# Queueing the state updates of linear attention as one alternating burst per half-head

## The chip, the cores and the metric

The kernel runs on one core of a Trainium2 chip. The metric is the device time of one execution, in microseconds (us). The chip's engines have queues of their own and meet only at semaphores: PE (TensorE, matrix products into PSUM), DVE (VectorE), ACT (ScalarE), POOL (GpSimd) and SP (SyncE, which here issues most of the transfers).

## The reference

Two layers of a hybrid encoder trunk on 512 frames of width 2048, all in float32. Each layer normalises its input, projects it with one wide matrix, and feeds two groups of heads: chunked softmax attention (8 heads of 128) and gated linear attention (4 heads, key width 128, value width 256). Gated outputs of both are concatenated, projected by `w_out`, normalised and added to the residual. The change concerns linear attention, which works in 8 chunks of 64 frames:

```python
L = jnp.cumsum(log_a..., axis=2)                 # inside a chunk
k_dec = kf * jnp.exp(L_end[:, :, None] - L)
U = jnp.einsum('bnchk,bnchv->bnhkv', k_dec, vf)  # one 128x256 update per chunk and head
A = jnp.exp(L_end)
new = a[..., None] * state + u                   # scan over the chunks
o = jnp.einsum('bnchk,bnhkv->bnchv', qf, states) # every frame reads its chunk's state
```

## The kernel before

The large projections run as matrix products on operands split into a high and a low part; each true product is kept as three (high·high, high·low, low·high). Weights are streamed from DRAM, ACT casts the high part (`wh`, L218), DVE subtracts the low part (`wl`, L223), and PE consumes them in jobs of 12 matmuls (in the blocks that save products, `fast_gemm`, L427 and L417) or 24 (`std_gemm`, L341). Between these, *tasks* add small work: attention, forget gates, linear attention, sums of operands for later products.

The program is built with a scheduler (the call passes `schedule_with_timeline_sim=True`): it decides, for each engine's queue, where an instruction stands, so the order of statements is only one of its inputs. `tc.issue_after(x)` makes what is recorded inside stand behind `x`. Engines then work through their queues strictly in that order, and a wait at the head of a queue holds all behind it.

Linear attention is cut into eight *units* per layer, one for a head `h` and a half `p` of the frames (256 frames, four chunks). `gla_heads` (behind the projection of the values, `gv_consume`) walks through two heads at a time. Units are numbered 0 to 7 here in the order in which they run: units 0 to 3 are heads 2 and 3, units 4 to 7 heads 0 and 1. For a unit:

- `outer` takes two PSUM banks, `ps_u[0]` and `ps_u[1]`, from a pool of four (`aux`), and forms the four chunk updates. A chunk has 64 frames, so its keys and values fill 64 of 128 partitions: chunk `cc` = 0 the lower half of the rows, `cc` = 1 the upper half. For each pair of chunks `tt` and each `cc`, three split products of 64 rows by 256 columns are accumulated into one half of bank `ps_u[cc]`: 12 matmuls (L1090).
- `states` is the scan on DVE: a copy (L1109) or four multiply-adds (L1111), which read the updates from PSUM.
- `read` has four matmuls of the queries with the states (L1124; each is unsplit float32 and shows as two in the trace) into a third bank.
- `norm` squares on ACT (L1134, L469) and takes a root on POOL (L465); `gate` multiplies on DVE (L1142); `turn`, delayed by some steps, transposes on PE (four matmuls, L1152) into another bank, which ACT copies out (L1163). Transfers then carry the result out and back for the sums of the output projection (L629, L655, L659; added on DVE at L622).

With four banks, the next `outer` waits until earlier banks have been read.

Of the kernel before, what the change touches and what calls it, by code (L numbers as in the profile page):

```python
# [34 lines left out]
def hybrid_trunk(  # L35
# [13 lines left out]
    nc = tc.nc  # L49
# [38 lines left out]
    def aux():  # L88
        return ps_ax.tile([P, 512], F32, tag="ax", name=nm("ax"))
# [620 lines left out]
    def layer(l):  # L710
# [359 lines left out]
        class Unit:  # L1070
# [5 lines left out]
            def outer(self):  # L1076
                h, p = self.h, self.p
                hk = slice(h * P, (h + 1) * P)
                hv = slice((h % 2) * 256, (h % 2 + 1) * 256)
                self.ps_u = [aux(), aux()]  # L1080
                for tt in range(2):
                    ops = []
                    for cc in range(2):
                        r = slice(cc * 64, (cc + 1) * 64)
                        kh, kl = kdh[p][r, tt, hk], kdl[p][r, tt, hk]
                        vh, vl = self.gvh[p][r, tt, hv], self.gvl[p][r, tt, hv]
                        ops.append(((kh, vh), (kh, vl), (kl, vh)))
                    for i in range(3):
                        for cc in range(2):
                            nc.tensor.matmul(  # L1090
                                self.ps_u[cc][:, tt * 256 : (tt + 1) * 256], ops[cc][i][0], ops[cc][i][1],
                                start=(i == 0), stop=(i == 2),
                            )

            def states(self):
                h, p = self.h, self.p
# [313 lines left out]
```

## Time and profile before

| what | value |
|---|---|
| time, median of 3 runs | 1637.59 us (1635.76 to 1638.52) |
| the profiled execution | 1637.15 us |
| its span | 1635.2 us |
| PE busy | 1625.8 us (99% of the span), 8990 matmuls |
| DVE, ACT, POOL busy | 1228.0, 904.6, 169.9 us |
| transfers | 469.59 MB, mean 287 GB/s |
| matmuls of `outer` (L1090) | 192, 26.5 us busy |

A matmul's busy time in the trace is longer than its share of PE, since matmuls overlap: two rows that follow each other start nearer together than the first one's duration. What a matmul costs is therefore read from the starts: the time from the start of one row to the start of a later one, divided among the instructions between them. A row of the timeline merges equal neighbours and gives their start, the time to the last one's end, and their count. Linear attention runs from about 590 to 690 us in the first layer and from about 1404 to 1504 us in the second.

### The profile page before, as it was taken

Reading aid. Unit: us, or ns where it says so; the run is one execution under the profiler, and the core shown is the slowest. Engines: PE = TensorE matmul, PEld = TensorE weight load, DVE = VectorE, ACT = ScalarE, POOL = GpSimd, SP = SyncE. Lnnn points to the kernel's source line nnn. Section 1 sums busy time; section 2 is a strip of 40 time slices with the busy share of each in tenths; the row PEclk is TensorE's granted clock in tenths of the full one; section 3 lists DMA queues with packets and bytes.
Section 4 is the critical chain, followed back from the end, with each engine's and each line's share of the span. In section 5 each row is a group of like instructions: output and inputs, shape, how many; then the busy total and the mean of one; then the engine's idle time right before and its main releaser. Section 6 shows DMA issues by size and latency. Waiting matters only on the chain.

```text
span 1635.2 us, 24844 instructions
## 1 busy us (share of the span) xinstructions
PE 1625.8 (99%) x8990; PEld 1392.6 (85%) x8990; DVE 1228.0 (75%) x1587; ACT 904.6 (55%) x1516; POOL 169.9 (10%) x259
## 2 busy tenths in 40 slices
PE   9999999999999999999999999999999999999998
PEld 7888889999978877788888888899999888777886
DVE  7567776877877886778886676768778778866887
ACT  8444544556676644555783445445566665445553
POOL 1210000001101201310122000000001012013100
PEclk9999999999999999999999999999999999999999
DMA  9979786858868696898789697968588676969986
GB/s 374 360 280 322 283 313 227 304 181 311 291 196 283 208 378 233 308 364 315 276 303 388 228 332 268 321 221 304 187 312 274 218 265 232 355 225 332 376 307 233
DMA packets 150778, 469.59 MB, mean 287 GB/s; under 512 B 16428, under 2 KB 35892, under 8 KB 150656
## 3 DMA queue, kind: packets, MB, share of 16 engines
q1 hardware_dynamic: 128064, 389.69, 68.1%
q0 software_dynamic: 22016, 77.37, 12.0%
q8 instruction: 71, 1.16, 0.3%
q10 hardware_dynamic: 576, 0.95, 0.2%
q14 instruction: 51, 0.42, 0.1%
HBM read 395.83 MB, written 71.06 MB: 286 GB/s over the span
## 4 chain that ended last, share of the span: by engine, by line
PE 99%; DMA 0%; DVE 0%; ACT 0%; SPq 0%; DVEq 0%; POOLq 0%; issue 0%
PE mm L427 46%; PE mm L341 22%; PE mm L417 20%; PE ax L920 2%; PE ax L1090 1%; PE ax L427 1%; PE ax L903 1%; PE ax L1124 1%; PE ax L745 1%; PE ax L882 1%; PE ax L883 1%; PE ax L881 1%; PE ax L1152 0%; PE ax L569 0%; PE ax L951 0%; DMA raw<-in_w_dram 0%
## 5 line engine op out<-in xcount | busy, mean ns | idle before, releaser
L427 PE MATMUL mm<-wh,sa 128*128 128x512 f32 x1536 | 485.1, 391 | 0.0
L218 ACT CAST wh<-raw 128x1024 fp32r<-128x1024 f32 x255 | 269.1, 1057 | 255.7 <-PE mm L427 115.8
L223 DVE TENSOR_TENSOR wl<-raw,wh 128x1024 fp32r<-128x1024 f32 (+1 forms) x257 | 312.3, 1217 | 125.5 <-PE mm L427 44.1
L218 ACT CAST wh<-H 128x1024 fp32r<-128x1024 f32 x224 | 235.3, 1053 | 217.6 <-PE mm L427 109.9
L223 DVE TENSOR_TENSOR wl<-H,wh 128x1024 fp32r<-128x1024 f32 x224 | 273.1, 1222 | 106.6 <-PE mm L427 46.4
L427 PEld LDWEIGHTS mm<-wh,sa 128*128 128x128 f32 x1536 | 287.9, 188 | 62.2 <-issue 1.5
L427 PE MATMUL mm<-wl,sa 128*128 128x512 f32 x768 | 299.9, 390 | 0.0
L417 PE MATMUL mm<-sa,wh 128*128 128x256 f32 x1280 | 237.3, 286 | 0.0
L417 PEld LDWEIGHTS mm<-sa,wh 128*128 128x128 f32 x1280 | 199.9, 191 | 0.3
L427 PE MATMUL mm<-wh,a 128*128 128x512 f32 x576 | 185.7, 393 | 0.0
L417 PE MATMUL mm<-sa,wl 128*128 128x256 f32 x640 | 180.6, 283 | 0.0
L427 PEld LDWEIGHTS mm<-wl,sa 128*128 128x128 f32 x768 | 144.3, 188 | 30.3
L341 PE MATMUL mm<-wh,a 128*128 128x512 f32 x512 | 167.4, 394 | 0.1
L207 DVE TENSOR_TENSOR H<-H,raw 128x1024 f32<-128x1024 f32 x120 | 145.9, 1220 | 3.5 <-DMA raw<-in_w_dram 1.8
L465 POOL TENSOR_TENSOR sm<-sm,mhalf 128x4 f32<-128x4 f32 (+2 forms) x40 | 60.6, 1514 | 777.7 <-DVE sm L936 550.8
L427 PEld LDWEIGHTS mm<-wh,a 128*128 128x128 f32 x576 | 107.9, 188 | 23.2 <-issue 0.8
L417 PEld LDWEIGHTS mm<-sa,wl 128*128 128x128 f32 x640 | 122.3, 191 | 0.1
L341 PEld LDWEIGHTS mm<-wh,a 128*128 128x128 f32 x512 | 96.0, 188 | 21.1 <-ACT wh L215 0.5
L427 PE MATMUL mm<-wl,a 128*128 128x512 f32 x288 | 113.0, 392 | 0.0
L341 PE MATMUL mm<-wl,a 128*128 128x512 f32 x256 | 100.1, 392 | 0.0
L417 PE MATMUL mm<-a,wh 128*128 128x256 f32 x512 | 94.9, 285 | 0.0
L341 PE MATMUL mm<-wh,sa 128*128 128x512 f32 x256 | 85.9, 394 | 0.0
(208 smaller groups left out, 2332.9 us busy)
## 6 DMA issues: line engine op xcount, KB each, us to landing
raw<-in_w_dram SPq DMA_DIRECT2D x319, 512.0 KB, 5.8
sa<-S SPq DMA_DIRECT2D x192, 512.0 KB, 4.7
H<-in_w_dram SPq DMA_DIRECT2D x56, 512.0 KB, 5.2
sa<-A SPq DMA_DIRECT2D x48, 512.0 KB, 6.1
S<-g POOLq DMA_DIRECT2D x32, 512.0 KB, 7.6
oS<-g POOLq DMA_DIRECT2D x32, 512.0 KB, 6.3
sa<-oS SPq DMA_DIRECT2D x32, 512.0 KB, 5.2
sg<-t POOLq DMA_DIRECT2D x32, 256.0 KB, 6.1
```

The costliest lines, as they stand in the source:

```text
L207: nc.vector.tensor_tensor(out=h, in0=h, in1=r, op=ALU.add)
L218: last_cast[0] = nc.scalar.copy(self.wh, src).ins
L223: last_low[0] = nc.vector.tensor_tensor(out=self.wl[:, kk, :], in0=self.src[:, kk, :], in1=self.wh[:, kk, :].bitcast(F32), op=ALU.subtract ...
L341: mm = nc.tensor.matmul(pss[o], a[:, part, t], rhs[:, kk, :], start=(i == 0 and kk == 0 and m == 0), stop=(i == n - 1 and kk == 1 and m == 2),
L417: nc.tensor.matmul(dst, lhs[:, kk, f], a[:, part, tok], start=(fresh and kk == 0 and m == 0 and ft % 2 == 0), stop=(c == c_last and kk == ...
L427: nc.tensor.matmul(out_ps[t], a[:, part, tok], rhs[:, kk, :], start=(fresh and kk == 0 and m == 0), stop=(c == c_last and kk == 1 and m == ...
L465: return nc.gpsimd.tensor_tensor(out=out_r, in0=v, in1=mhalf[:, : v.shape[-1]], op=ALU.pow).ins
L745: nc.tensor.matmul(ps[0:96, half * 256 : (half + 1) * 256], wga[kt // 10][:, kt % 10, :], op[:, i, (kt % 2) * 256 : (kt % 2 + 1) * 256], s ...
L881: nc.tensor.matmul(ps[:, :n], self.qh[:, t], self.kh[:, :n], start=True, stop=False)
L882: nc.tensor.matmul(ps[:, :n], self.qh[:, t], self.kl[:, :n], start=False, stop=False)
L883: nc.tensor.matmul(ps[:, :n], self.ql[:, t], self.kh[:, :n], start=False, stop=True)
L920: nc.tensor.matmul(o, self.pt[i][:, j * P : (j + 1) * P], av[hd // 4, j // 2][:, j % 2, (hd % 4) * P : (hd % 4 + 1) * P], start=(j == 0), ...
```

## The change

Only `Unit.outer` changes.

```diff
                 self.ps_u = [aux(), aux()]
-                for tt in range(2):
+                nc.vector.memset(self.ps_u[0][:, 0:1], 0.0)
+                mm = None
+                for tt in (1, 0):
                     ops = []
                     for cc in range(2):
...
-                        ops.append(((kh, vh), (kh, vl), (kl, vh)))
+                        ops.append(((kh, vl), (kl, vh), (kh, vh)))
                     for i in range(3):
-                        for cc in range(2):
-                            nc.tensor.matmul(
-                                self.ps_u[cc][:, tt * 256 : (tt + 1) * 256], ops[cc][i][0], ops[cc][i][1],
-                                start=(i == 0), stop=(i == 2),
-                            )
+                        for cc in (1, 0):
+                            with tc.issue_after(mm) if mm else nullcontext():
+                                mm = nc.tensor.matmul(
+                                    self.ps_u[cc][:, tt * 256 : (tt + 1) * 256], ops[cc][i][0], ops[cc][i][1],
+                                    start=(i == 0), stop=(i == 2),
+                                ).ins
```

The same 12 products are formed. Each is recorded behind the one before it, so that the scheduler must keep them in a row that alternates the halves, upper half first, the later pair of chunks first. A new DVE instruction, a memset of one column of `ps_u[0]`, stands ahead: the first matmul into `ps_u[0]`, the second of the twelve, waits for it, and the memset itself waits until the bank's former content has been read. The source lines behind it move by 3: L1090 becomes L1093, L1109 L1112, L1111 L1114, L1124 L1127, L1142 L1145, L1152 L1155, L1163 L1166.

On PE, unit 6 of the first layer before. `ax_6679` is its `ps_u[0]`, `ax_6680` its `ps_u[1]`; the rows shown begin with the end of six matmuls into the first bank, and six into the second follow behind the last row, ahead of the read of unit 5:

```order
L1090 MATMUL ax_6679<-g_1197_6347,g_1028_5572 128x256
L1090 MATMUL ax_6679<-g_1196_6346,g_1030_5574 128x256
L341 MATMUL mm_6545<-wh_6530,a_1154_6143 128x512
L341 MATMUL mm_6545<-wl_6638,a_1154_6143 128x512
L341 MATMUL mm_6545<-wh_6530,a_1154_6143 128x512
L341 MATMUL mm_6546<-wh_6530,sa_6486 128x512
L341 MATMUL mm_6546<-wl_6638,sa_6486 128x512
L341 MATMUL mm_6546<-wh_6530,sa_6486 128x512 x2
L341 MATMUL mm_6546<-wl_6638,sa_6486 128x512
L341 MATMUL mm_6546<-wh_6530,sa_6486 128x512
L341 MATMUL mm_6547<-wh_6530,sa_6486 128x512
L1090 MATMUL ax_6680<-g_1196_6346,g_1028_5572 128x256
```

The same unit now (`ax_6685` is `ps_u[0]`, `ax_6686` is `ps_u[1]`), from its fourth matmul on:

```order
L1093 MATMUL ax_6685<-g_1196_6349,g_1030_5574 128x256
L1093 MATMUL ax_6686<-g_1196_6349,g_1028_5572 128x256
L1093 MATMUL ax_6685<-g_1196_6349,g_1028_5572 128x256
L1093 MATMUL ax_6686<-g_1197_6350,g_1028_5572 128x256
L1093 MATMUL ax_6685<-g_1197_6350,g_1028_5572 128x256
L1093 MATMUL ax_6686<-g_1196_6349,g_1030_5574 128x256
L1093 MATMUL ax_6685<-g_1196_6349,g_1030_5574 128x256
L1093 MATMUL ax_6686<-g_1196_6349,g_1028_5572 128x256
L1093 MATMUL ax_6685<-g_1196_6349,g_1028_5572 128x256
L1127 MATMUL ax_6723<-g_1262_6606,g_976_5334 64x256 x4
L1155 MATMUL ax_6740<-cst,bias_6592 128x128 x4
L341 MATMUL mm_6548<-wl_6717,a_1153_6141 128x512
```

Two runs of six on one half each have become one run of twelve; behind it stand the read of unit 5 and the transposes of unit 4 without a projection matmul between them.

On DVE, around unit 2 of the first layer before (`g_1188` is its state, `wl` the low parts of weights):

```order
L1109 COPY g_1188_6306<-ax_6307 128x256
L385 SCALAR_TENSOR_TENSOR t_1195_6344<-mm_5723,norm_208,ev_5840 128x512
L1142 SCALAR_TENSOR_TENSOR bias_6227<-ax_6266,sm_6278,bias_6227 128x256 x2
L223 TENSOR_TENSOR wl_6338<-H_5639,wh_6300 128x1024
L1111 SCALAR_TENSOR_TENSOR g_1188_6306<-g_1188_6306,a_end_254,ax_6308 128x256
L109 TENSOR_TENSOR g_1197_6347<-t_1195_6344,g_1196_6346 128x512
L385 SCALAR_TENSOR_TENSOR t_1198_6350<-mm_5724,norm_208,ev_5842 128x512
L1111 SCALAR_TENSOR_TENSOR g_1188_6306<-g_1188_6306,a_end_254,ax_6307 128x256
```

and now:

```order
L109 TENSOR_TENSOR g_1197_6350<-t_1195_6347,g_1196_6349 128x512
L1112 COPY g_1188_6308<-ax_6309 128x256
L109 TENSOR_TENSOR g_1197_6350<-t_1198_6353,g_1196_6349 128x512
L1114 SCALAR_TENSOR_TENSOR g_1188_6308<-g_1188_6308,a_end_254,ax_6310 128x256
L1114 SCALAR_TENSOR_TENSOR g_1188_6308<-g_1188_6308,a_end_254,ax_6309 128x256
L1114 SCALAR_TENSOR_TENSOR g_1188_6308<-g_1188_6308,a_end_254,ax_6310 128x256
L1081 MEMSET ax_6407 128x1
L223 TENSOR_TENSOR wl_6398<-H_5669,wh_6343 128x1024
```

The state steps of a unit stand together, and the memset for the next unit's bank (`ax_6407`, unit 3) stands behind them and ahead of a weight job's low part.

## The prediction

> **What bounds the kernel now.** I read the page's chain of work that ended last, then PE's waits over the whole run, then PE's timeline in the stage of the change.
>
> ```profile
> PE 99%; DMA 0%; DVE 0%; ACT 0%; SPq 0%; DVEq 0%; POOLq 0%; issue 0%
> ```
>
> ```profile
> PE ax L674 <- DVE t L671: 1.2, 1, 1.2
> ```
>
> The chain that ends last is PE from end to end, and the only wait that the trace names for PE is the first matmul's. So a microsecond that PE needs less comes off the end, as long as no new wait appears; and busy time on other engines costs nothing. What is left to ask is what PE pays for the stage that the change touches. Since matmuls overlap, I price by the distance of starts. First an ordinary matmul of 512 columns:
>
> ```profile
> 591.65 0.61 PE L427 MATMUL mm<-wh,sa 128*128 128x512 f32 x2
> 592.11 0.39 PE L427 MATMUL mm<-wl,sa 128*128 128x512 f32 x1
> 592.34 0.61 PE L427 MATMUL mm<-wh,sa 128*128 128x512 f32 x2
> 592.79 0.39 PE L427 MATMUL mm<-wl,sa 128*128 128x512 f32 x1
> ```
>
> Five starts in 1.14 us: 0.228 each. Now a run of six matmuls of L1090 that alternates the row halves, and one of six on a single half; each with the matmul ahead of it and two behind it, because the entry and the exit cost too:
>
> ```profile
> 602.92 0.39 PE L427 MATMUL mm<-wh,a 128*128 128x512 f32 x1
> 603.24 0.62 PE L1090 MATMUL ax<-g,g 64*128 64x256 f32 x6
> 603.79 0.50 PE L427 MATMUL mm<-wh,a 128*128 128x512 f32 x1
> 604.12 0.40 PE L427 MATMUL mm<-wl,a 128*128 128x512 f32 x1
> ...
> 625.12 0.39 PE L427 MATMUL mm<-wh,sa 128*128 128x512 f32 x1
> 625.43 0.97 PE L1090 MATMUL ax<-g,g 64*128 64x256 f32 x6
> 626.33 0.50 PE L427 MATMUL mm<-wh,sa 128*128 128x512 f32 x1
> 626.67 0.40 PE L427 MATMUL mm<-wl,sa 128*128 128x512 f32 x1
> 626.90 0.39 PE L427 MATMUL mm<-wh,sa 128*128 128x512 f32 x1
> 627.22 0.98 PE L1090 MATMUL ax<-g,g 64*128 64x256 f32 x6
> 628.13 1.08 PE L1124 MATMUL ax<-g,g 128*64 128x256 f32 x8
> 629.14 0.50 PE L427 MATMUL mm<-wh,sa 128*128 128x512 f32 x1
> 629.48 0.39 PE L427 MATMUL mm<-wl,sa 128*128 128x512 f32 x1
> ```
>
> From 602.92 to 604.12 are 1.20 us, less two ordinary starts (0.456): 0.744 for six alternating. From 625.12 to 626.67 are 1.55: 1.094 for six on one half. Two halves overlap, so six alternating take three slots and six alike take six; three slots are 0.351, **0.117 a slot**, and what is left, 0.744 - 0.351 = 0.393, is the price of **one separate run**. The last five rows hold six alike and a read (L1124, eight rows) in one visit: 2.58 - 0.456 = 2.124. A read alone:
>
> ```profile
> 633.36 0.40 PE L427 MATMUL mm<-wl,sa 128*128 128x512 f32 x1
> 633.69 1.08 PE L1124 MATMUL ax<-g,g 128*64 128x256 f32 x8
> 634.70 0.50 PE L427 MATMUL mm<-wh,sa 128*128 128x512 f32 x1
> 635.04 0.40 PE L341 MATMUL mm<-wh,a 128*128 128x512 f32 x1
> ```
>
> 1.68 - 0.456 = 1.224; so a read **directly behind** a run saves 1.094 + 1.224 - 2.124 = 0.194.
>
> **The change part by part.** No matmul is added or removed. (a) *Overlap.* Counting the runs of L1090 in the first layer's order and in the timeline, unit by unit, the 96 matmuls take 7, 6, 12, 12, 7, 12, 12 and 6 slots: 74. In four units the scheduler had put the halves into runs of their own, which cannot overlap. Now seven to six slots each: 51 (three units are still cut once, and an odd run wastes a slot). A run of twelve exists before:
>
> ```profile
> 663.46 0.99 PE L1090 MATMUL ax<-g,g 64*128 64x256 f32 x12
> ```
>
> 0.99 us for twelve against 0.97 for six alike: six slots, whatever their number. 23 slots by 0.117 are 2.69 us. (b) *Runs.* 17 separate runs of L1090 become 11; six by 0.393 are 2.36. (c) *A read in two pieces.* Unit 0's read stands in two places before:
>
> ```profile
> 610.55 1.08 PE L1124 MATMUL ax<-g,g 128*64 128x256 f32 x6
> ...
> 613.06 0.40 PE L427 MATMUL mm<-wl,a 128*128 128x512 f32 x1
> 613.39 0.65 PE L1124 MATMUL ax<-g,g 128*64 128x256 f32 x2
> 613.97 0.97 PE L1090 MATMUL ax<-g,g 64*128 64x256 f32 x6
> 614.87 0.72 PE L427 MATMUL mm<-wh,a 128*128 128x512 f32 x2
> 615.43 0.39 PE L427 MATMUL mm<-wl,a 128*128 128x512 f32 x1
> ```
>
> Six of eight take the 1.08 us that a whole read takes; the other two, ahead of six alike, cost 2.37 - 3 x 0.228 - 1.094 = 0.592, and 0.786 without the neighbour's saving. Now the read is whole: 0.79. (d) *Neighbours.* Runs with a read directly behind or ahead are 5 before, 6 now: 0.19. (e) *Transposes behind the read.* Four reads per layer are now followed by L1152's four transposes. No row shows that transition; between a gain like (d)'s, 0.19, and a loss of a switch's like size, 0.1, I take nothing, since it is one switch for another: 4 x 2 layers give -1.6 to +0.8 us in all.
>
> The sum is 2.69 + 2.36 + 0.79 + 0.19 = 6.03 us per layer. Both layers' stages, by windows (us; PE, PEld, DVE, ACT, POOL busy with counts; clock; transfer share; GB/s):
>
> ```profile
> 590.00:690.00 100.00, 100.00 (x507) 74.18 (x506) 70.58 (x107) 47.31 (x99) 19.91 (x31) 1.00 0.79 286
> 1404.00:1504.00 100.00, 100.00 (x507) 74.17 (x506) 71.82 (x109) 47.55 (x100) 19.57 (x30) 1.00 0.80 286
> ```
>
> PE does the same 507 matmuls in 100 us of the second, in the same order, so the saving counts twice, 12.1: 1637.15 - 12.1 = **1625.0 us**. The profiled execution lies 0.4 below the median; I leave that inside the range.
>
> The Trainium skill's TensorEngine Tiling (Array Packing), section Key Properties, says that changing the tiling mode drains TensorE; its TensorE: Matmul & The Clock Gate, section Single matmul latency, puts a drain at about 175 ns. (b) to (d) remove 15 changes of mode per layer (47 to 32, two per run less one per neighbour). By that figure, an estimate, they would be worth 2.6 us per layer instead of the rows' 3.34, and the time 1626.5; by the rows a removed change is worth 0.22 us, so the trace agrees in kind and is somewhat above it.
>
> (f) *The memset.* The nearest row, from the groups:
>
> ```profile
> L862 DVE MEMSET bias<- 64x64 f32 x16 | 1.8, 112 | 6.2 <-DMA bias<-in_rel_dram 6.1
> ```
>
> Eight by 0.112 are 0.9 us per layer on DVE, which is busy for 70.6 of the stage's 100 us: free as work, and 1.8 us in all if the cover were gone. Its danger is its place. DVE keeps its order, so a memset that waits for a bank holds the low parts of weights (L223) behind it; and PE, which also keeps its order, stands at the second matmul of a burst until the memset is through. In the order that I read, each memset that waits stands behind the instructions of its own engine that free the bank, or (unit 5's) waits for ACT's copy of unit 2's transposes, which stand 19 matmuls, 4.3 us, ahead of PE's next use of DVE's work at that place, unit 3's transposes. So I charge nothing.
>
> (g) *Waits that come nearer.* The tightest that I find is unit 6's burst: it needs a bank that unit 5's third update reads, and that update stands on DVE behind a sum (L622) of loaded operands. Before:
>
> ```profile
> 644.21 0.55 PE L1152 MATMUL ax<-cst,sg 128*128 128x128 f32 x3
> ...
> 616.76 0.87 DVE L1142 SCALAR_TENSOR_TENSOR bias<-ax,sm,bias 128x256 f32<-128x256 f32 x2
> 653.59 0.69 DVE L622 TENSOR_TENSOR t<-t,t 128x512 f32<-128x512 f32 x1 [2.84 <-DMA t<-fg]
> 654.20 1.51 DVE L1111 SCALAR_TENSOR_TENSOR g<-g,a_end,ax 128x256 f32<-128x256 f32 x3
> ...
> L223 DVE TENSOR_TENSOR wl<-raw,wh 128x1024 fp32r<-128x1024 f32 (+1 forms) x257 | 312.3, 1217 | 125.5 <-PE mm L427 44.1
> ```
>
> From the end of unit 3's transposes, behind which SP issues those loads, to the sum are 653.59 - 644.76 = 8.8 us; the sum and three updates end at 655.7, 10.9 us behind the transposes. In the new order unit 6's burst stands 42 ordinary matmuls (9.6), a burst (0.7) and a burst with a read (2.1) behind the same transposes: 12.4. Slack 1.5 us. Elsewhere a burst follows a read and about 22 matmuls behind the one before, 6 us, in which DVE does two low parts (2 x 1.22, L223), a gate (0.87, L1142) and four updates (4 x 0.50, L1111), 5.3 us: it fits, with under a microsecond over if all of it has to come first.
>
> **The rivals.** *Waits give part back.* If PE waits half a microsecond at seven units of each layer, 7 of the 12.1 us are lost: 1632, from 1627 to 1634 for a quarter and for three quarters of it. For it: the slacks above are one to two microseconds, and transfers vary. Against: PE waited for nothing with DVE just as full.
>
> *Transfers take the lead back.* Directly behind the stage:
>
> ```profile
> 690.00:780.00 90.00, 90.00 (x398) 74.22 (x397) 72.59 (x79) 46.04 (x66) 9.12 (x17) 1.00 0.94 341
> ...
> SPq L156 <- DVE wl L223: 18.8, 9, 5.7
> ```
>
> The transfer engines are 94% busy there at 341 GB/s, against 79% and 286 in the stage. If they set the pace, arriving 6 us early only means waiting: 1637. Against it the second row, SP's longest wait from 690 to 740 us: for 18.8 of 50 us it holds weight loads until DVE frees a buffer, so the queue follows the engines.
>
> *The burst doesn't overlap.* If twelve in a row took twelve slots, (a) would turn into a loss of 22 x 0.117 = 2.6 per layer against (b) to (d)'s 3.34: 1635.6. The row of twelve speaks against it.
>
> *The banks become a ring that stops PE: slower.* With four banks, a burst waits for the unit before last to be squared, scaled and gated; the scheduler, if it expects those sooner than they come, puts each burst too early. After the second piece of unit 0's read (end 614.04) the gate's row (616.76 and 0.87) ends 3.6 us later. Paid in full at 16 units that is 57.6 - 12.1, so 1683; it turns the sign from 12.1/16 = 0.76 us per unit. Against: 20 or more matmuls stand between bursts, 4.6 us.
>
> **How the numbers follow.** Forecast 0.68; waits give part back 0.14; transfers 0.07; no overlap 0.05; ring 0.06. A change under 0.2% (3.3 us) can't be told from none here. Faster: 0.68 + 0.14 less the 0.01 of the second that ends above 1634, 0.81. Same: 0.07 + 0.05 + 0.01, 0.13. Slower 0.06. The forecast's own bounds, (e) and the run-to-run difference, are 1623 to 1627; to hold eight in ten the range reaches below by a gain at each transition and above over most of the second case: 1622 to 1634.
>
> **What would show it.** L1093 should have rows of x12 with 0.95 to 1.0 us, or x1 and x11, where six alike stood; its count 192; PE's waits should still name nothing in 590 to 690 us; the stages behind should start 6 and then 12 us earlier. A wait of PE for DVE's memset (L1081) or update (L1114) means the first or the last rival; PE waiting for `wl` behind a memset, the last; PE waits after 690 us, the transfers. I am wrong if the sum of starts over the stage falls by 6 and the end doesn't.

## The result and the profile after

| | before | after |
|---|---|---|
| time, median of 6 each | 1637.79 us (1635.76 to 1638.52) | 1624.59 us (1623.82 to 1625.67) |
| ratio | | 0.9922, 95% interval 0.9909 to 0.9934 |
| the profiled execution, its span | 1637.15, 1635.2 us | 1624.68, 1622.9 us |
| predicted | | 1625.0 us, range 1622 to 1634 |

The kernel is 13.2 us (0.8%) faster, and the prediction holds to 0.4 us. A later measurement of the same kernel gave 1624.98 us beside 1636.52 us before (change_b below). The gain of 12.1 us that was forecast lies between the two that were measured, 13.2 and 11.5 us, so the 0.4 us is partly luck.

The page's chain of work that ended last, and PE's waits over the whole execution (engine, line, releaser: us in total, times, longest):

```profile
PE 98%; DMA 1%; ACT 0%; DVE 0%; issue 0%; DVEq 0%; POOLq 0%; ACTq 0%
```

```profile
PE ax L674 <- DVE t L671: 1.2, 1, 1.2
PE mm L341 <- DVE wl L223: 0.5, 1, 0.5
PE ax L1036 <- DVE t L385: 0.3, 1, 0.3
```

PE is still the chain, but no longer alone in its list of waits: 0.5 us for a low part of weights and 0.3 us elsewhere are new. The first of them matters below. In PE's timeline unit 1's burst, with the read of unit 0 behind it, and a part of unit 7's burst with the read of unit 6 and the transposes of unit 5 (start, length, then the tile and shape):

```profile
606.81 0.61 PE L427 MATMUL mm<-wh,a 128*128 128x512 f32 x2
607.36 0.98 PE L1093 MATMUL ax<-g,g 64*128 64x256 f32 x12
608.26 1.08 PE L1127 MATMUL ax<-g,g 128*64 128x256 f32 x8
609.28 0.50 PE L427 MATMUL mm<-wl,a 128*128 128x512 f32 x1
609.61 0.63 PE L427 MATMUL mm<-wh,a 128*128 128x512 f32 x2
...
660.83 0.98 PE L1093 MATMUL ax<-g,g 64*128 64x256 f32 x11
661.74 1.08 PE L1127 MATMUL ax<-g,g 128*64 128x256 f32 x8
662.75 0.66 PE L1155 MATMUL ax<-cst,sg 128*128 128x128 f32 x4
```

Twelve matmuls, or eleven, take 0.98 us, which is what six on one half took before. The matmul ahead of the first visit starts at 607.04 (the second of the x2) and the second behind it at 609.61, so the visit costs 2.57 less two ordinary starts, 2.12 us. Doing this for every stretch of linear attention's matmuls (L1093, L1127 and L1155, between ordinary ones), with every distance counted once, gives what PE pays for linear attention: 28.51 us per layer before, 22.26 after, the same in both layers. I call this sum *the visits* below. The difference, 6.25 by two layers, is 12.5 us; the two spans differ by 12.3.

By windows (columns as in the prediction), the first with the borders used before and the second 6 us earlier:

```profile
590.00:690.00 100.00, 100.00 (x534) 76.77 (x533) 74.91 (x119) 50.93 (x107) 21.64 (x33) 1.00 0.85 308
1398.00:1498.00 100.00, 100.00 (x535) 76.77 (x534) 74.37 (x119) 50.45 (x106) 21.62 (x33) 1.00 0.86 307
```

PE begins 534 matmuls where it began 507: 27 ordinary ones at 0.228 us are 6.2 us. The clock is 1.00 as before. DVE is busier (74.9 against 70.6 us) because work of the next stage has moved up into the window. The memset, from the groups:

```profile
L1081 DVE MEMSET ax<- 128x1 f32 x16 | 0.9, 59 | 1.9 <-ACT t L1166 1.7
```

59 ns each, and a wait of 1.7 us in all for the copy behind a unit's transposes, on DVE, which nobody on PE paid for.

### The profile page after: what moved, and what is told of

It is laid out like the page before. It is cut to its first block, busy times and chain, and to the rows that moved or that the text cites. A ratio compares the mean times of both kernels' runs of the same rounds, so it can differ in the third digit from the quotient of the medians.

```text
span 1622.9 us, 24845 instructions
## 1 busy us (share of the span) xinstructions
PE 1612.6 (99%) x8990; PEld 1386.6 (85%) x8990; DVE 1230.1 (76%) x1603; ACT 906.0 (56%) x1516; POOL 167.5 (10%) x259
## 3 DMA queue, kind: packets, MB, share of 16 engines
q0 software_dynamic: 22016, 77.37, 12.3%
## 4 chain that ended last, share of the span: by engine, by line
PE 98%; DMA 1%; ACT 0%; DVE 0%; issue 0%; DVEq 0%; POOLq 0%; ACTq 0%
PE mm L427 46%; PE mm L341 21%; PE mm L417 20%; PE ax L920 2%; PE ax L427 1%; PE ax L903 1%; PE ax L1093 1%; PE ax L1127 1%; PE ax L745 1%; DMA t<-fg 1%; PE ax L882 1%; PE ax L883 1%; PE ax L881 1%; PE ax L1155 1%; PE ax L569 0%; PE ax L951 0%
## 5 line engine op out<-in xcount | busy, mean ns | idle before, releaser
L218 ACT CAST wh<-raw 128x1024 fp32r<-128x1024 f32 x255 | 269.1, 1057 | 258.5 <-PE mm L427 107.2
L218 ACT CAST wh<-H 128x1024 fp32r<-128x1024 f32 x224 | 235.4, 1053 | 214.9 <-PE mm L427 107.8
```

Source lines behind the costliest of these rows:

```text
L218: last_cast[0] = nc.scalar.copy(self.wh, src).ins
```

## The experiments

Twelve runs followed, of which change_b and g4_b repeat the change and g4. "Visits" is the sum defined above for both layers, against 57.0 us before. "Waits" are PE's named waits other than the first matmul's. The last column is the difference of medians to the kernel before, timed beside each.

| run | visits | waits in the trace | span against 1635.2 | time, difference to before |
|---|---|---|---|---|
| the change | -12.5 | 0.8 | -12.3 | 1624.59, -13.2 |
| grouped (six and six) | -8.7 | 1.1 | -7.4 | 1628.17, -8.6 |
| g5 (five, five, one, one) | -10.4 | 0.3 | -11.2 | 1625.75, -11.0 (one execution) |
| grouped3 (three and three) | -13.0 | 0.4 | -13.5 | 1623.88, -12.9 |
| g4 (four, four, two, two) | -14.0 | 0.5 | -14.4 | 1622.37, -14.4 |
| chainonly | -4.1 | 0.4 | -2.5 | 1635.59, -1.2 |
| nomemset | -11.2 | 1.5 | -9.6 | 1627.20, -9.6 |
| revonly | -6.2 | 7.6 | +4.2 | 1641.98, +5.2 |
| rev_pool | -6.2 | 1.6 | -4.2 | 1632.22, -4.5 |
| both37 | -14.1 | 4.8 | -7.1 | 1630.11, -6.7 |
| b37_pool | -14.1 | 4.6 | -7.5 | 1628.15, -8.5 |
| change_b | -12.5 | 0 | -13.4 | 1624.98, -11.5 |
| g4_b | -14.0 | 2.6 | -12.5 | 1622.63, -13.9 |

Visits plus waits give the span's difference to within 1.2 us, except in revonly, both37 and b37_pool, which lose 2.8, 2.2 and 2.0 us more. What is missing there is the clock. Two of revonly's windows, behind a wait and three microseconds later (columns as in the prediction, the clock third from the end):

```profile
711.00:713.00 2.00, 2.00 (x5) 1.61 (x6) 2.00 (x4) 2.00 (x3) 0.54 (x1) 0.50 1.05 400
714.00:716.00 2.00, 2.00 (x10) 1.63 (x10) 2.00 (x2) 1.14 (x2) 0.00 (x0) 1.00 1.04 414
```

PE stood for 3.5 us up to 709.74; from 710.48 to 713.90 its granted clock is 0.50, and six ordinary matmuls start 0.42 us apart instead of 0.228. The same happens once more in revonly, in the second layer, once in both37 (from 704.69 us) and once in b37_pool (from 1517.61), for 3.4 us each, and costs 1.2 to 1.4 us each time. With it the sums hold to 1.2 us everywhere. So a wait on PE can cost more than its own length. (Revonly's 9.2 us of waits in an expectation below were counted from the starts.)

One source of the remaining spread lies ahead of everything that was changed. In the two executions of the same kernel g4 and g4_b, the first and the second of these rows respectively stand at the start of the projection:

```profile
5.17 0.87 PE L341 MATMUL mm<-wh,a 128*128 128x512 f32 x2
```

```profile
5.51 0.73 PE L341 MATMUL mm<-wh,a 128*128 128x512 f32 x2 [0.67 <-ACT a L108]
```

By the starts, the same ordinary matmul at about 104 us comes 0.36 us later in the second than in the first; the rest of the 1.9 us between the two spans is lost at 579 us (0.3), behind the first stage (0.5) and at 852 us (0.8). A single span is therefore good to about 2 us; the visits repeat to 0.01 us from one execution to the next and decide where the times don't.

### Does the order of the twelve matter?

The prediction's term (a) counted slots by the larger of the two halves' counts in a run. It leaned on a row of twelve, at 663.46 us before, whose queue holds four of one half, four of the other and then two pairs. Had only neighbours in the queue overlapped, that row would have been longer. Four sequences tell the two readings apart; the memset and the chain stay.

```diff
-                for tt in (1, 0):
-                    for i in range(3):
-                        for cc in (1, 0):
+                for cc in (1, 0):           # grouped
+                    for tt in (1, 0):
+                        for i in range(3):
```

> The change's kernel with the same twelve matmuls of each unit still in one chained run, but all six of the upper half first and then all six of the lower half. On PE the same visits remain, except that units 3 and 7 are now whole (9 runs of L1093 per layer instead of 11). Theory 'the alternation does it' (a matmul starts beside the one ahead of it in the queue only if that one uses the other half): 88 slots per layer instead of 51, two runs fewer; 37 x 0.117 - 4 changes x 0.196 = +3.5 us per layer, so 7.1 us slower than the change, about 1631.7, and a run of twelve takes 1.5 to 1.6 us. Theory 'it is enough that both halves are queued together' (each half works through its own share, which the row of twelve at 663.46 us of the kernel before suggests, since its queue holds four, four and then two pairs): 53 slots, about 1 us per layer less than the change through the two runs saved, about 1623, and a run of twelve still takes 0.95 to 1.0 us.

```diff
-                    for i in range(3):
-                        for cc in (1, 0):
+                    for cc in (1, 0):       # grouped3
+                        for i in range(3):
```

> As the run above, but three of one half, three of the other, and again. By the alternation theory 73 slots and 10 runs per layer: +2.2 us per layer against the change, about 1629.0, with a run of twelve at 1.2 to 1.3 us. By the other theory 52 slots: about 1624.0, with a run of twelve at 0.95 to 1.0 us. If PE reaches ahead only a little way, this run is as fast as the change and the run above is not.

For the other two the halves follow a list; within each half the products keep their sequence.

```diff
+                todo = [[(tt, i) for tt in (1, 0) for i in range(3)] for _ in range(2)]
+                for cc in (1, 1, 1, 1, 0, 0, 0, 0, 1, 1, 0, 0):   # g4
+                    tt, i = todo[cc].pop(0)
...
+                for cc in (1, 1, 1, 1, 1, 0, 0, 0, 0, 0, 1, 0):   # g5
```

> The change with the twelve of a unit in one chained run, in the sequence four of the upper half, four of the lower, two and two: the sequence that the scheduler had given unit 7 before the change, now in every unit. In the run of three and three each half's first matmul started beside the other's; in the run of six and six the lower half's first started beside the third of the upper, four places ahead of its turn. Theory 'PE reaches four matmuls ahead': all pair up, 51 slots and a run of twelve at 0.95 to 1.0 us; as units 3 and 7 stand whole, 28 changes of mode per layer instead of 32: 0.8 us per layer less than the change, about 1623.0, unless a wait behind the stage takes it back (then 1624 to 1626). Theory 'it reaches three ahead': one slot more per unit at least, a run of twelve at 1.1 us, about 1625.

> As the run above with five, five, one and one. By a reach of four the first of the upper half starts alone and then pairs begin: 7 slots, or 8 if loads come late, so that a run of twelve takes 1.07 to 1.2 us and its second start lies 0.22 us behind the first without a partner. By a longer reach 6 slots, 0.95 to 1.0 us.

The burst of unit 1 in the timelines of grouped, g5, g4 and grouped3, in this sequence:

```profile
608.28 1.32 PE L1094 MATMUL ax<-g,g 64*128 64x256 f32 x12
```

```profile
607.75 1.20 PE L1094 MATMUL ax<-g,g 64*128 64x256 f32 x12
```

```profile
606.82 0.98 PE L1094 MATMUL ax<-g,g 64*128 64x256 f32 x12
```

```profile
607.54 0.98 PE L1094 MATMUL ax<-g,g 64*128 64x256 f32 x12
```

Three and three, and four and four, are as short as strict alternation; five and five cost 0.22 us more; six and six 0.34. Neither theory for grouped was right: 1628.2 lies between 1623 and 1631.7. The distances of the twelve starts in that burst (us, from the trace's records) show what happens:

```
alternating  .003 .219 .004 .115 .004 .113 .003 .115 .004 .116 .003
3 and 3      .010 .213 .010 .109 .010 .107 .010 .108 .010 .109 .010
4, 4, 2, 2   .014 .209 .014 .105 .012 .105 .013 .105 .012 .107 .011
5, 5, 1, 1   .223 .007 .112 .111 .005 .114 .005 .111 .008 .111 .119
6 and 6      .223 .119 .007 .110 .111 .007 .111 .008 .112 .120 .120
```

A distance under 0.015 us is a pair. Six pairs in the first three, four in the fourth (8 slots), three in the last (9 slots); two and three slots of 0.117 more than six are the 0.22 and 0.34 us. In the kernel before, the six of a run on one half never start nearer than 0.11 us, so a pair has one of each half. In six and six the first pair is the third and fourth to start, and the fourth is the lower half's first: of the twelve records only the first and the fourth last 0.38 us, which the first on a half does, and the others 0.28. Six of the upper half stand ahead of it in the queue, and only three have started: it went past three waiting matmuls. In five and five it starts third and in four and four second, each time past three. A semaphore says the same without the durations: the first matmul into `ps_u[0]`, the lower half's first, is the one that has to wait for DVE's memset, and in four units of each layer the weight load with a wait for DVE's semaphore stands 1 to 2 ns ahead of the second start in four and four, of the third in five and five, of the fourth in six and six. So PE takes matmuls for the idle half out of turn, past at most three that wait for the other. The Trainium skill's TensorE: Matmul & The Clock Gate, section The mechanism, says that matmuls start and end strictly in the queue's order; these starts differ, unless something rearranges the queue behind the program, which no row here shows. The sentence ahead of the prediction that engines work through their queues strictly in order is likewise too strong for PE.

For the change this means that strict alternation is not what pays. It pays that both halves' matmuls stand in one run, no more than four of a half in a row.

### Runs and overlap, one without the other

```diff
-                nc.vector.memset(self.ps_u[0][:, 0:1], 0.0)
-                for tt in (1, 0):
+                for tt in range(2):
-                        ops.append(((kh, vl), (kl, vh), (kh, vh)))
+                        ops.append(((kh, vh), (kh, vl), (kl, vh)))
-                        for cc in (1, 0):
+                        for cc in range(2):
```

> The kernel before with the chain alone: each matmul of L1090 recorded behind the one before it, in the old sequence (first pair of chunks first, lower half first, high by high first) and without the memset. The halves alternate in every unit (55 slots per layer, 74 before, 51 with the change), but the bursts remain cut: 18 separate runs of L1090 per layer as before (17), 48 changes of mode (47 before, 32 with the change). If overlap and runs are priced rightly, overlap alone returns: 19 x 0.117 = 2.2 less 0.2 for a change of mode, 2.0 us per layer, 4 us in all: about 1633.2. If the overlap were worth nothing and all of the gain came from fewer visits, no change: 1637. If overlap were all of it, 1626.

The visits fall by 4.1 us, where the prices gave 4.0. So the overlap's price is right, and the larger part of the change's gain belongs to the fewer visits. Single pairs and single matmuls now stand alone, which prices a visit directly:

```profile
605.17 0.63 PE L427 MATMUL mm<-wh,a 128*128 128x512 f32 x2
605.73 0.39 PE L1093 MATMUL ax<-g,g 64*128 64x256 f32 x2
606.04 0.50 PE L427 MATMUL mm<-wl,a 128*128 128x512 f32 x1
606.38 0.62 PE L427 MATMUL mm<-wh,a 128*128 128x512 f32 x2
```

From 605.40 (the second of the x2) to 606.38 are 0.98 us, less 0.455: 0.526 for one slot, and lone matmuls elsewhere in this trace cost 0.51. One slot and one run by the prediction's prices are 0.117 + 0.393 = 0.51. The time, though, fell by 1.2 us only, in ten executions spread from 1634.45 to 1639.14; ratio 0.9996 (0.9987 to 1.0006). The profiled execution is the fastest of the ten; by its starts it loses 0.55 us at the low part behind the first stage. Where the slower ones lose theirs no trace tells, and this stays open.

### The sequence of statements alone, and the memset

```diff
-                nc.vector.memset(self.ps_u[0][:, 0:1], 0.0)
-                            with tc.issue_after(mm) if mm else nullcontext():
```

revonly leaves out both of these lines, nomemset the first.

> The change's sequence alone (later pair of chunks first, upper half first, high by high last), without the chain and without the memset. The queue then holds 12 runs of L1092 per layer (17 before, 11 with the change), but units 3, 5 and 6 are still put as six of one half and six of the other with other work or nothing between: 62 slots (74, 51) and 36 changes of mode (47, 32). By the prices (0.117 and 0.196): 12 x 0.117 + 11 x 0.196 = 3.6 us per layer less than before, 7.1 in all: about 1630. So more than half of the gain would come from the sequence of statements alone. If the chain is what matters, 1636 or above.

> The change without the memset: sequence and chain stay. 51 slots and 33 changes of mode per layer (51 and 32 with it); three bursts are cut into 1 and 11, of which two lone matmuls stand behind other work of the stage. Theory 'the memset costs nothing and does almost nothing': +0.2 us per layer, about 1625.0. If the memset's place on DVE costs PE something (the small waits of 0.3 and 0.5 us that the change's trace shows), 1624 or below; if the memset is what holds the bursts together, 1628 or above.

Revonly is the sharpest miss: its visits fall by 6.2 us (7.1 priced), and it is *slower* than before by 0.3% (ratio 1.0030, 1.0019 to 1.0041). PE's waits and the rows behind the first layer's stage:

```profile
PE mm L341 <- ACT wh L218: 6.1, 2, 3.5
...
PE mm L341 <- DVE wl L223: 1.1, 2, 0.5
```

```profile
690.68 0.33 SPq L659 DMA_DIRECT2D t<-fg  x1
...
706.72 1.42 DVE L622 TENSOR_TENSOR t<-t,t 128x512 f32<-128x512 f32 x2 [7.54 <-DMA t<-fg]
...
708.64 1.04 ACT L218 CAST wh<-raw 128x1024 fp32r<-128x1024 f32 x1 [0.58 <-DMA raw<-in_w_dram]
...
709.72 1.22 DVE L223 TENSOR_TENSOR wl<-raw,wh 128x1024 fp32r<-128x1024 f32 x1 [0.20 <-ACT wh L218]
...
709.74 0.73 PE L341 MATMUL mm<-wh,a 128*128 128x512 f32 x2 [3.49 <-ACT wh L218]
```

This is where the output projection's sums begin. SP issues the load of the second of linear attention's results for these sums (`t<-fg`, L659; two more follow later) at 690.68; the sum that needs it (L622) begins 16.0 us later; behind it on DVE stands the low part of the next weights, and ACT's next high part (L218) waits behind a cast (L108) of the sum. PE stands still for both. The results are not the only late load: the cast ends at 708.07, and ACT waits 0.58 us more for the weights themselves. SP had issued them at 691.63, just behind the results, and they landed at 708.54, after 16.9 us; their load in the change took 11.7 (688.48 to 700.16).

Nomemset, at 1627.20, is 2.2 us above change_b's 1624.98: visits of 1.35 us more (three bursts cut in 1 and 11, a read in two) and the same kind of wait, 0.9 + 0.6 us. Its five executions, 1625.73 to 1628.76, overlap in part with the change's. So the memset costs nothing and is worth about 2 us, by where it makes the scheduler put things.

### The wait behind the stage

Both37 was to save a little more: a second memset makes the first matmul of units 3 and 7 wait too.

```diff
                 nc.vector.memset(self.ps_u[0][:, 0:1], 0.0)
+                if h % 2 and p:
+                    nc.vector.memset(self.ps_u[1][:, 0:1], 0.0)
```

> The change with a second memset, on the other bank, in units 3 and 7 alone: their first matmul now waits as the second does, and their bursts, cut into 1 and 11 by the change, stand whole. 49 slots instead of 51 and 29 changes of mode instead of 32 per layer: 2 x 0.117 + 3 x 0.196 = 0.8 us per layer, 1.6 in all: 1623.0. If those two first matmuls only filled time in which PE would wait, the wait appears in its place and the time is the change's 1624.6 or above.

Its visits do fall by 1.6 us more than the change's, as priced, but PE waits 4.8 us, 3.7 of them at the same place as revonly:

```profile
686.47 0.33 SPq L659 DMA_DIRECT2D t<-fg  x1
...
700.22 1.42 DVE L622 TENSOR_TENSOR t<-t,t 128x512 f32<-128x512 f32 x2 [5.25 <-DMA t<-fg]
703.53 1.22 DVE L223 TENSOR_TENSOR wl<-raw,wh 128x1024 fp32r<-128x1024 f32 x1
...
703.29 0.74 PE L341 MATMUL mm<-wh,a 128*128 128x512 f32 x2 [1.25 <-ACT wh L218]
704.80 0.79 PE L341 MATMUL mm<-wl,a 128*128 128x512 f32 x1 [0.78 <-DVE wl L223]
```

The change itself, in the first layer and in the second:

```profile
687.53 0.34 SPq L659 DMA_DIRECT2D t<-fg  x1
698.95 1.42 DVE L622 TENSOR_TENSOR t<-t,t 128x512 f32<-128x512 f32 x2 [2.92 <-DMA t<-fg]
701.66 1.22 DVE L223 TENSOR_TENSOR wl<-raw,wh 128x1024 fp32r<-128x1024 f32 x1
703.39 0.39 PE L341 MATMUL mm<-wl,a 128*128 128x512 f32 x1
...
1507.55 1.42 DVE L622 TENSOR_TENSOR t<-t,t 128x512 f32<-128x512 f32 x2 [4.07 <-DMA t<-fg]
1510.26 1.22 DVE L223 TENSOR_TENSOR wl<-raw,wh 128x1024 fp32r<-128x1024 f32 x1
1511.53 0.50 PE L341 MATMUL mm<-wl,a 128*128 128x512 f32 x1 [0.54 <-DVE wl L223]
```

In the first layer the low part ends at 702.88 and PE takes it at 703.39: half a microsecond to spare. In the second it ends at 1511.48 and PE has waited 0.54 us. The kernel before stood just as close:

```profile
694.03 0.33 SPq L659 DMA_DIRECT2D t<-fg  x1
...
705.94 1.42 DVE L622 TENSOR_TENSOR t<-t,t 128x512 f32<-128x512 f32 x2 [3.41 <-DMA t<-fg]
...
708.66 1.22 DVE L223 TENSOR_TENSOR wl<-raw,wh 128x1024 fp32r<-128x1024 f32 x1
...
709.93 0.50 PE L341 MATMUL mm<-wl,a 128*128 128x512 f32 x1
```

The low part ends at 709.88, and PE takes it at 709.93. No wait was named there, and there was no slack either. The load took 11.9 us from issue to sum before (694.03 to 705.94) and 11.4 after (687.53 to 698.95): the change kept its whole gain because this load was issued 6.5 us sooner and took no longer, so that the sum came sooner too, by 7.0 us.

Is it the queue in which the load stands? One edit, in both37 and in revonly, has POOL issue these loads:

```diff
-                nc.sync.dma_start(tiles[2 * half + 1], of_gla[l][half, c])
+                nc.gpsimd.dma_start(tiles[2 * half + 1], of_gla[l][half, c])
```

> The kernel of run revonly (sequence of statements alone; 1642.0 where 1630 was forecast, with 9.2 us of PE's waits behind the stages, and L622 beginning 16.0 us behind the issue of its load) with the same edit: the loads t<-fg on POOL's queue. By the first theory the time falls to what the starts in the stages give, 1630 to 1632; by the second it stays at 1642. If it falls by a part only, the sequence delays something else too.

> The kernel of run both37 (whole bursts in units 3 and 7; 1630.1 where 1623.0 was forecast, PE standing 6.1 us behind the stages) with one edit elsewhere: the loads of linear attention's results for the sums (t<-fg) are issued by POOL instead of SP, whose queue carries the weight loads. PE's queue hardly changes. In both37 the last of them was issued at 686.47 us and the sum that needs it (L622) began at 700.22, with low parts of weights (L223) behind it on DVE. Theory 'the load stands behind weight loads in its queue': it lands 4 us sooner or more, the wait of L622 goes, PE's waits at 702 to 706 and at 1514 to 1516 us with it, and the time is 1623 to 1625. Theory 'the transfer engines are full, whatever the queue': no earlier landing, 1630. If POOL's own waits (for sums to be cast) delay the issue: slower than 1630.

rev_pool behaves as the first theory says: 1632.2 instead of 1642.0, PE's waits 1.6 instead of 7.6 us. The load is issued later and the sum still begins sooner:

```profile
695.03 0.54 POOL L659 DMA_DIRECT2D t<-fg  x1 [0.41 <-ACT wh L218]
...
705.56 1.42 DVE L622 TENSOR_TENSOR t<-t,t 128x512 f32<-128x512 f32 x2 [0.55 <-DMA t<-fg]
```

10.5 us instead of 16.0, and L622's wait has shrunk from 7.5 to 0.55 us. With it the sequence alone gains what its visits say (-6.2 + 1.6, against -4.5 measured). In b37_pool it is half a success: 1628.15 instead of 1630.11. The first layer's wait shrinks, but one of 3.2 us stands in the second:

```profile
PE mm L341 <- ACT wh L218: 3.5, 2, 3.2
```

```profile
700.15 1.05 ACT L218 CAST wh<-raw 128x1024 fp32r<-128x1024 f32 x1 [7.97 <-DMA raw<-in_w_dram]
...
1514.36 0.69 DVE L622 TENSOR_TENSOR t<-t,t 128x512 f32<-128x512 f32 x1 [3.51 <-DMA t<-fg]
...
1515.09 0.62 ACT L108 CAST g<-t 128x512 fp32r<-128x512 f32 x1 [5.50 <-DVE t L622]
```

Now the weights come late as well, and in the second layer the load again. So the wait is one for transfers, shown by rev_pool; that the queue alone decides it is not shown, since b37_pool keeps a part of it. Why the same load takes 11.4 us (the change), 11.9 (before), 13.8 (both37) or 16.0 (revonly) behind nearly the same work stays open.

### The change beside the faster sequence

> The change itself once more, beside the run of four and four below on the same chip, so that the two can be told apart: 1624.6 as before, and the same sum of starts, 45.5 us for all visits of L1093, L1127 and L1155 in both layers.

> The run of four, four, two and two again (1622.4 before; its visits cost 43.6 us by the starts, 1.9 less than the change's). If the starts carry the end, 1.5 to 2.3 us below the run of the change beside it; if the difference between the two earlier numbers was one between chips or days, none.

On one chip, five executions each: 1624.98 (1623.59 to 1626.89) and 1622.63 (1621.96 to 1624.49). Over both measurements, eleven executions of the change lie from 1623.59 to 1626.89 and nine of g4 from 1621.93 to 1624.49. The expectations' sums, 45.5 and 43.6, count a distance twice where a single ordinary matmul lies between two visits; counted once they are 44.5 and 43.0. Four, four, two and two is 2.3 us faster than the change, of which its cheaper visits explain 1.5: its bursts of units 3 and 7 come out whole, four runs fewer over both layers. Against the kernel before its ratio is 0.9915 (0.9902 to 0.9928). The profiled execution of g4_b was its slowest, with 0.7 us lost at the place behind the stage:

```profile
699.59 1.42 DVE L622 TENSOR_TENSOR t<-t,t 128x512 f32<-128x512 f32 x2 [4.29 <-DMA t<-fg]
...
703.58 0.50 PE L341 MATMUL mm<-wl,a 128*128 128x512 f32 x1 [0.74 <-DVE wl L223]
```

## Why the prediction was right, point by point

- **The bound.** Right: PE's visits went from 57.0 to 44.5 us, and the span followed, 12.3 for 12.5. The step from "no wait is named" to "a microsecond less on PE comes off the end" was too quick, though: at 709.9 us PE had 0.05 us to spare, and revonly and both37 show 6.2 and 14.1 us of visits saved turning into +5.2 and -6.7 us of time.
- **(a) to (d), overlap, runs, the read, neighbours.** The sum was 6.03 us per layer, and the visits fell by 6.25, of which 0.22 belong to (e). That the rest agrees to the hundredth is luck, since each price is read to 0.01 us and counts many times. The slots and runs counted from the order are those of the trace. The prices were tested apart: overlap by chainonly (4.0 forecast, 4.1 measured), a lone run by its single matmuls (0.51 forecast and measured). By the 175 ns that the Trainium skill's TensorE: Matmul & The Clock Gate, section Single matmul latency, gives for a drain, (a) to (d) would have been, as an estimate, 2.69 + 2.6 = 5.3 per layer. The visits are nearer to the rows' 0.22.
- **(a), its ground.** "A row of twelve exists" was good evidence, and for a reason that the prediction didn't state: that row's queue did not alternate. PE reaches past three waiting matmuls, so overlap needs the halves to be near each other, not to alternate.
- **(e) Transposes behind a read.** Taken as nothing within -1.6 to +0.8 in all; no row stood behind the 0.1 of the upper bound. A visit of twelve, a read and four transposes costs 2.510, without the transposes 2.120; four transposes alone 0.446. The neighbour saves 0.056 us, four times per layer: -0.45 in all.
- **(f) The memset.** Free as work, as forecast; 59 ns rather than the 112 taken from the nearest row. No wait of PE for it appears. What the prediction missed is that it helps, by about 2 us (nomemset): the order in which it counted runs, neighbours and whole reads is one that the memset had helped to make.
- **(g) The tightest wait.** This step failed. It named unit 6's burst with 1.5 us of slack; PE waited there for nothing. The tightest place lay behind the stage, at the first sum of the output projection, and there it was 0.5 us in the first layer and a wait of 0.5 us in the second.
- **The rivals.** "Waits give part back" took 0.8 us of the profiled execution and none in change_b's, far from the 7 it was priced at, but neighbours of the change lost 7 to 11 us there. Its bounds, 1627 to 1634, don't share one base: a quarter and three quarters of the 7 us give 1626.8 and 1630.3, of the whole 12.1 us 1628.0 and 1634.1. "Transfers take the lead back" named the right stretch, and the argument against it was too quick: SP's weight loads are issued as DVE frees their buffers, but in revonly the weights and the results that SP issued at about 691 us both took 16 to 17 us to come. "The burst doesn't overlap" is refuted by the row of 0.98 us. "The ring" did not appear as a wait of PE at any burst; no kernel with a longer memset was run, so its price is not tested.

## What to carry to other kernels

Price short foreign visits on PE by starts, with their entry and exit: here a lone run of the 64-row matmuls cost 0.39 us beside its slots, and gathering visits was worth more than half of the gain. Before trusting such a sum, look for the next place where PE takes something just in time, even where no wait is named: the same few microseconds came off the end in one order and were lost at one load in another. And where two kinds of small matmuls can share PE, it is enough to queue them close together, here no more than four of one kind in a row; the sequence can then be chosen for what the scheduler makes of it.

## What was not expected of the hardware

- PE starts a matmul for the idle half of its rows ahead of up to three matmuls that wait for the other half: 0.98 us for twelve in four and four, 1.20 in five and five, 1.32 in six and six.
- The transposes behind a read save 0.056 us, less than a third of the 0.194 that a read behind a burst saves.
- A 256 KB load behind the stage took 11.4 us from issue to use in one order (the change) and 16.0 in another (revonly), with the transfer engines 94 to 96% busy from 684 to 780 us in both.
- Behind waits of PE of 3.5 us (revonly), 3.2 (b37_pool) and 1.25 with 0.78 (both37), the granted clock stood at 0.50 for 3.4 us, which cost another 1.2 to 1.4 us each. Behind 0.9 with 0.8 us (both37, second layer) it stayed at 1.00.
